# A streaming Conformer layer on one core: VectorE's work is counted with other durations, and block 0's stores are fewer and later

## The chip, the cores and the metric

The kernel runs on one core of a Trainium2 chip. The core has TensorE (PE, matrix products; PEld is its loading of weights), VectorE (DVE), ScalarE (ACT), GpSimd (POOL) and SyncE (SP, which here only issues DMAs); each works through its own list of instructions in order and waits for the others by semaphores. The metric is the device time of one execution in microseconds (us); lower is better.

## The reference, cut to what matters

One layer over a prompt of 2048 tokens and a sample of 32 tokens, all in float32. One projection of the modulated RMSNorm of x feeds two branches, which are gated, added, projected and normed again.

```python
h = rms_norm(x, g_pre) * (1 + scale) + shift            # shift, scale, gate = split(c @ w_mod + b_mod)
a, b, z_conv, q, k, v, z_attn, g_conv, g_attn = split(h @ w_in)
u = a * sigmoid(b)
y = depthwise_conv(u, dw_w, width 31) + dw_b            # per channel, causal; 512 channels
y_conv = (silu(layer_norm(y, ln_g, ln_b)) * silu(z_conv)) @ w_conv_out
o = band_attention(q, k, v, rel_bias)                   # 8 heads of 64, chunks of 64, 8 past chunks
y_attn = (o * silu(z_attn)) @ w_attn_out
merged = sigmoid(g_conv) * y_conv + sigmoid(g_attn) * y_attn
out = x + gate * rms_norm(merged @ w_o, g_post)
```

## The kernel before, in words

Float32 products are made of three products of halves (`mm3`): each operand is split into a rounded part (`wh`, by ACT) and the rest (`wl`, a subtraction on DVE or POOL). The 2048 tokens are taken in four blocks of 512; block 0 also carries the 32 sample tokens, so its matmuls have 272 columns twice where the others have 512. Channels lie on partitions.

A block goes through these stages. **v**: the value projection (`vS`, `vT`). **Attention**: scores (`sps`, `sa`), softmax (`sp`, `mn`, `ll`), transposes (`pt`, `pth`, `ptl`), products (`pv`); between them `fill` places the other projections (`pj`), in the order that `FILL(b)` lists: q and k of the heads, a and b of the convolution in block 0, z, and in block 0 also eight pieces m0 to m7 of the gate row (`mod_part`, `gate_row`). **Gate stage**: sixteen gate projections (`pj`, columns C_GC and C_GA) and four times two products with w_attn_out (`py<-ah`). **Merge stage**: eight products with w_conv_out (`py<-cohi,w`), each behind four transposes of the next block's x (`pxt`). Then w_o in two halves, with the next block's a and b between them.

The convolution's 31 taps for four channel groups are 124 DVE instructions a block (`y<-u,dww,y`, generator `conv`). After the last tap comes a chain: `norm_conv` adds the four groups on POOL (`u<-y`), halves the sum (`lnhi` on ACT, `lnlo` on DVE), takes the mean on PE (`pmean`), subtracts it (`y<-y,pmean`), squares and adds (ACT, POOL), halves again, takes the second `pmean`, forms the reciprocal root on DVE (`rsqrt`, the `u<-u` rows) and multiplies on POOL (`y<-y,u`); then `co` makes tanh and affine on ACT (`th`, `xn`), two products on DVE, and the halves `cohi` (ACT) and `colo` (DVE), which the merge stage reads.

The program writes out each engine's list itself. Two counters decide where a tap stands: `pace.pe` sums an estimate of each matmul as it is written, `pace.dve` (class `Vec`) one of each DVE instruction, and `tick` places taps as long as `pace.dve <= pace.pe + pace.lead`. The norm chain's steps start at times of `pace.pe` too (`YL`). After the gate stage the program writes out what is left of the taps, the chain and `co`, and only then the merge stage. SP's list is not written out by hand; the scheduler orders its DMAs.

Weights come in tiles (`plan`). `weights(i)` splits tile i+2 (`w_parts`, L226 and L228), loads tile i+4 (`w_load`, L216, buffers `raw`) and stores the halves of tile i+1 to DRAM (`w_keep`, L236, 1 MB, on ACT's queue) if it is used again; later blocks load those (`w<-kept`). Which use stores it is `keep_at`. `spill_v` (L603) stores v for the next block.

Of the kernel before, what the change touches and what calls it, by code (L numbers as in the profile page):

```python
# [8 lines left out]
F32 = mybir.dt.float32  # L9
F32R = mybir.dt.float32r  # L10
# [6 lines left out]
P = 128  # L17
D = 1024
# [3 lines left out]
TB = 512  # L22
# [10 lines left out]
C_A, C_B, C_ZC, C_Q, C_K, C_V, C_ZA, C_GC, C_GA = (  # L33
    0, 512, 1024, 1536, 2048, 2560, 3072, 3584, 4608)
# [10 lines left out]
DV = -0.5  # L45
# [8 lines left out]
def FILL(b):  # L54

    part = dict(q=C_Q, k=C_K, a=C_A, b=C_B, z=C_ZA, c=C_ZC, m=C_MOD)
    order = "b0 a0 q1 m0 k1 m1 b1 m2 a1 m3 b2 q2 m4 k2 m5 a2 m6 z0 m7 b3 a3 z1 q3 k3 z2 z3 c0 c1 c2 c3" if b == 0 else \
        "q1 k1 z0 q2 k2 z1 q3 k3 z2 z3 c0 c1 c2 c3"
    return [(int(x[1]), part[x[0]]) for x in order.split()]


def dram(ap, off, dims):
    return bass.AP(tensor=ap.tensor, offset=ap.offset + off, ap=[list(d) for d in dims])
# [54 lines left out]
class Vec:  # L118
# [5 lines left out]
    def __getattr__(self, name):  # L124
        fn = getattr(self.nc.vector, name)

        def call(out, *a, **k):
            n = 1
            for d in out.shape[1:]:
                n *= d  # L130
            ns = 60 + n * (0.6 if name in ("tensor_scalar", "tensor_copy", "memset") else 1.05)
            if name == "scalar_tensor_tensor":
                ns += 70
            ns = max(ns, 200)
            self.pace.dve = max(self.pace.dve, self.pace.pe) + ns / 1e3
            return fn(out, *a, **k)  # L136
        return call
# [3 lines left out]
def mixer_kernel(ctx, tc, x_prompt, x_sample, c_prompt, c_sample, cache_conv, cache_k, cache_v,  # L141
# [4 lines left out]
    G = nc.gpsimd  # L146
    pace = Pace()
    V = Vec(nc, pace)

    def mm(out, lhsT, rhs, start, stop):  # L150
        n = 1
        for d in rhs.shape[1:]:
            n *= d
        pace.pe += (6 + n * 0.4063) / 1e3
        nc.tensor.matmul(out, lhsT=lhsT, rhs=rhs, start=start, stop=stop)  # L155
# [6 lines left out]
    wp = ctx.enter_context(tc.tile_pool(name="wp", bufs=2))  # L162
# [6 lines left out]
    def pp_tile(name):  # L169
        return pp.tile([P, 512], F32, tag="pp", name=name)  # L170
# [18 lines left out]
    for b in range(NB):  # L189
        plan += [w_wide("v", w_in, k, C_V) for k in range(0, KT, 2)]  # L190
        plan += [w_fill(n, c) for n, c in [(0, C_Q), (0, C_K)] + FILL(b)]
        for m in range(0, KT, 2):
            for i in range(2):
                plan += [w_cols(c + (m + i) * P) for c in (C_GC, C_GA)]
            plan.append(w_half("ao", w_attn_out, m))
        plan += [w_half("co", w_conv_out, m) for m in range(0, KT, 2)]
        plan += [w_wide("o", w_o, k, 0) for k in range(0, KT, 2)]
        if b < NB - 1:
            plan += [w_cols(c + ct * P) for ct in range(NCT) for c in (C_B, C_A)]
        plan += [w_wide("o", w_o, k, 512) for k in range(0, KT, 2)]  # L200

    uses = {}
    for i, entry in enumerate(plan):
        uses.setdefault(entry[0], []).append(i)
    keep_at = {key: at[1 if key[0] == "v" else 0] for key, at in uses.items()}
    again = {key for key, at in uses.items() if len(at) > 1}
    raws, halves, kept, used = {}, {}, {}, [0]

# [7 lines left out]
    def w_parts(i):  # L218

        if i < len(plan):  # L220
            key = plan[i][0]
            w = wp.tile([P, 2, 1024], F32R, tag="w", name="w", bufs=3)
            wh, wl = w[:, 0], w[:, 1]
            if i <= keep_at[key]:
                raw = raws.pop(i)
                act(wh, raw, AF.Copy)  # L226
                on_v = pace.dense or pace.idle is None and pace.dve <= pace.pe + DV
                (V if on_v else G).tensor_tensor(wl, raw, wh.bitcast(F32), op=OP.subtract)  # L228
            else:
                nc.sync.dma_start(w.bitcast(F32), kept[key])  # L230
            halves[i] = w
# [6 lines left out]
    def weights(key):  # L238
        i = used[0]
        assert plan[i][0] == key, (i, plan[i][0], key)  # L240
        used[0] += 1
        w_parts(i + 2)
        w_load(i + 4)
        w_keep(i + 1)
        w = halves.pop(i).rearrange("p h (k c) -> p h k c", c=plan[i][1])
        return w[:, 0], w[:, 1]
# [240 lines left out]
    def shape(b):  # L487
        yw = TB + (HIST + TS if b == 0 else 0)
        return TB + (TS if b == 0 else 0), yw, [(0, TB, 0)] + ([(USEP0, USEP0 + TS, TB)] if b == 0 else [])
# [74 lines left out]
    def mod_part(i):  # L564


        n, kp = i // 4, i % 4
        m4, bm, gr = aof[0:4, 3, 0:512], aof[0:2, 2, 0:512], aof[0:2, 1, 0:512]
        if kp == 0:
            nc.sync.dma_start(bm, dram(b_mod, 2 * D + n * 512, [[0, 2], [1, 512]]))  # L570
            nc.sync.dma_start(gr, dram(g_post, n * 512, [[0, 2], [1, 512]]))
        wh, wl = weights(("mod", 2 * kp, (4 + n) * 512))
        pm = pp_tile("pm")
        for kk in range(2):
            mm(pm[0:4], c4[:, 2 * kp + kk, :], wh[:, kk, :], kk == 0, False)
            mm(pm[0:4], c4[:, 2 * kp + kk, :], wl[:, kk, :], False, kk == 1)
            yield
        if kp == 0:
            act(m4, pm[0:4], AF.Copy)
        else:  # L580
            V.tensor_tensor(m4, pm[0:4], m4, op=OP.add)
        if kp == 3:
            pace.start(gate_row(n, m4, bm, gr), 1.5)

    def gate_row(n, m4, bm, gr):
        pg = pp_tile("pg")
        nc.tensor.matmul(pg[0:2], lhsT=sel, rhs=m4, start=True, stop=True)
        yield 1.5
        V.tensor_tensor(bm, pg[0:2], bm, op=OP.add)
        V.tensor_tensor(bm, bm, gr, op=OP.mult)  # L590
        nc.sync.dma_start(gp_d[:, n * 512:(n + 1) * 512], bm)
        gate_done.add(n)
        yield 0.0
# [7 lines left out]
    def spill_v(b, vcur):  # L601
        for t in range(4):
            nc.sync.dma_start(vs_d[b][:, t], vcur[:, t].bitcast(F32))  # L603
            yield 6.0
# [20 lines left out]
    with tc.tile_pool(name="init", bufs=1) as ini:  # L625
        mraw, mparts, m4 = {}, {}, {}
# [63 lines left out]
        with tc.tile_pool(name="x0", bufs=5) as x0:  # L690
# [31 lines left out]
            c2 = vecs[:, 0:16].rearrange("p (a k) -> p k a", a=2)  # L722
# [79 lines left out]
    qls = []  # L802
    for b in range(NB):
        NT, YW, ypieces = shape(b)
# [4 lines left out]
        with tc.tile_pool(name="at", bufs=1) as at:  # L809
# [3 lines left out]
            vcur = at.tile([P, 4, H, P], F32R, name="vcur")  # L813
# [22 lines left out]
                    o = (nvs[0, 0, 512 - TS:512] if t == 4 else nvp[0, 0, t * P:(t + 1) * P])  # L836
                    nc.sync.dma_start(o.rearrange("t h d -> t (h d)"), vo[0:m, 0:512])
            if b < NB - 1:
                pace.start(spill_v(b, vcur), 30.0)

            if b < 2:

                qls.clear()
                for _ in range(2):
                    qls.append(wp.tile([P, 2, TB], F32R, tag="raw", name="ql0") if b else
                               at.tile([P, 2, NT], F32R, tag="ql", name="ql", bufs=2))
                    G.memset(qls[-1][64:128, 0].bitcast(F32), 0.0)
                    G.memset(qls[-1][0:64, 1].bitcast(F32), 0.0)


            att, cvs, ready = {}, {}, set()
# [595 lines left out]
```

## Time and profile before

| | |
|---|---|
| median of three runs | 1754.84 us (1751.86 to 1756.65) |
| the profiled execution | 1752.31 us, of which its span (first to last instruction) 1750.5 us |
| PE busy | 1676.9 us, 96% of the span |
| PE's weight loads | 1428.5 us, 82% |
| DVE, ACT, POOL busy | 1122.5, 633.5, 234.6 us |
| mean granted clock | 0.988 of full speed |

PE is busy nearly all the time, so the profile is read for the stretches in which it is not, and for what ends each of them. The stages can be told by what PE runs: block 0's attention lies at 75 to 330 us of the span, its gate stage at 330 to 458; block 1's gate stage at 761 to 873, block 2's at 1161 to 1272.

### The profile page before, as it was taken

The numbers are of one execution on the slowest core, as the hardware profiler recorded it, in microseconds if no ns is written. First come the engines' busy times: TensorE is split into PE (matmuls) and PEld (weight loads), VectorE is DVE, ScalarE is ACT, GpSimd is POOL, SyncE is SP. The second block draws the span as 40 slices with busy tenths as digits, with TensorE's granted clock in tenths as the row PEclk, the third lists the DMA queues.
The fourth block names the chain that finished last, engine by engine and source line by source line (L and its number), as shares of the span: only waits on it lengthen the run. The fifth ranks groups of instructions, "written<-read, shape, count | busy, mean of one in ns | idle before, by whom it ended". The sixth has DMA issues, their size and how long they took to land.

```text
span 1750.5 us, 23607 instructions
## 1 busy us (share of the span) xinstructions
PE 1676.9 (96%) x9221; PEld 1428.5 (82%) x9221; DVE 1122.5 (64%) x2030; ACT 633.5 (36%) x1218; POOL 234.6 (13%) x174
## 2 busy tenths in 40 slices
PE   6978889999999999999999999999999999999997
PEld 4767779999878788888788888888888888888886
DVE  6457878796737867674544967774543967665423
ACT  6544534424721255522331045531330045531211
POOL 5423332101310000001120000001120000001120
PEclk9998999999999999999999999999999999999999
DMA  8786455776675774465455674465555674455553
GB/s 271 238 286 227 164 200 207 263 277 224 235 261 207 269 276 167 148 226 190 172 217 182 236 272 179 153 221 190 181 216 188 220 262 150 148 181 195 189 192 144
DMA packets 132326, 368.61 MB, mean 211 GB/s; under 512 B 9326, under 2 KB 75050, under 8 KB 101975
## 3 DMA queue, kind: packets, MB, share of 16 engines
q1 hardware_dynamic: 123575, 304.19, 50.4%
q10 hardware_dynamic: 8640, 62.92, 8.8%
q8 instruction: 73, 1.20, 0.3%
q14 instruction: 38, 0.31, 0.1%
HBM read 280.41 MB, written 91.77 MB: 213 GB/s over the span
## 4 chain that ended last, share of the span: by engine, by line
PE 73%; DVE 4%; ACT 2%; DMA 1%; issue 1%; POOL 0%; POOLq 0%; ACTq 0%; DVEq 0%
PE pj L155 41%; PE py L155 9%; PE pv L155 4%; PE op L155 3%; PE sps L155 3%; PE pt L159 3%; PE oT L155 3%; PE oS L155 3%; PE vS L155 2%; PE vT L155 2%; PE oP L155 1%; DMA raw<-in_w_in_dram 1%; DVE pre L136 1%; DMA raw<-in_w_attn_out_dram 1%; PE pxt L159 0%
## 5 line engine op out<-in xcount | busy, mean ns | idle before, releaser
L155 PE MATMUL pj<-hh,w 128*128 128x512 f32 (+1 forms) x4800 | 975.9, 357 | 12.7 <-DVE kk L136 5.4
L155 PEld LDWEIGHTS pj<-hh,w 128*128 128x128 f32 x4800 | 782.6, 190 | 134.7 <-ACT kk L863 4.9
L136 DVE SCALAR_TENSOR_TENSOR y<-u,dww,y 128x512 f32<-128x512 f32 (+1 forms) x480 | 345.9, 781 | 0.5
L1084 ACT ACTIVATE sp<-sp,mn 128x640 f32<-128x640 f32 (+5 forms) x136 | 103.6, 762 | 133.9 <-DVE mn L136 133.9
L1119 ACT ACTIVATE pth<-pt 128x256 fp32r<-128x256 f32 (+4 forms) x184 | 91.8, 500 | 135.1 <-PE pt L159 123.7
L136 DVE TENSOR_TENSOR ptl<-pt,pth 128x256 fp32r<-128x256 f32 (+4 forms) x184 | 104.0, 565 | 28.1 <-ACT pth L1119 26.7
L228 POOL TENSOR_TENSOR w<-raw,w 128x1024 fp32r<-128x1024 f32 x37 | 92.2, 2497 | 177.3 <-ACT w L226 147.7
L136 DVE CUSTOM_DVE_ANT_0 sp<-sps,bias 128x640 f32<-128x640 f32 (+4 forms) x128 | 94.1, 735 | 26.5 <-PE sps L155 25.5
L155 PE MATMUL py<-ah,w 128*128 128x512 f32 (+1 forms) x480 | 96.0, 356 | 6.9 <-DVE t L136 4.8
L226 ACT ACTIVATE w<-raw 128x1024 fp32r<-128x1024 f32 x72 | 75.7, 1052 | 70.5 <-PE py L155 17.0
L155 PEld LDWEIGHTS py<-ah,w 128*128 128x128 f32 x480 | 79.8, 192 | 20.5 <-DVE t L136 5.2
L159 PE MATMUL pt<-ident,sp 128*128 128x128 f32 (+1 forms) x600 | 95.2, 274 | 0.0
L155 PE MATMUL py<-cohi,w 128*128 128x512 f32 (+1 forms) x320 | 90.1, 357 | 1.6 <-DVE mg L136 1.6
L532 POOL TENSOR_TENSOR u<-y 128x512 f32<-128x512 f32 (+1 forms) x4 | 5.3, 1324 | 641.5 <-DVE y L136 591.0
L136 DVE TENSOR_SCALAR sp<-sp,ll 128x640 f32<-128x640 f32 (+5 forms) x136 | 84.5, 621 | 4.8
L155 PE MATMUL sps<-kk,qh 128*128 128x320 f32 (+1 forms) x224 | 70.3, 321 | 9.1 <-DVE mn L136 8.3
L159 PEld LDWEIGHTS pt<-ident,sp 128*128 128x128 f32 (+1 forms) x600 | 69.6, 141 | 3.6 <-issue 1.3
L1347 POOL TENSOR_TENSOR mg<-mg,t 128x512 f32<-128x512 f32 (+1 forms) x32 | 46.4, 1451 | 172.2 <-issue 118.8
L155 PE MATMUL sps<-kk,ql 128*128 128x320 f32 (+1 forms) x224 | 68.5, 313 | 0.0
L1311 ACT ACTIVATE t<-pj 128x512 f32<-128x512 f32 (+1 forms) x40 | 20.7, 517 | 127.6 <-PE pj L155 127.4
L136 DVE SCALAR_TENSOR_TENSOR t<-t,py 128x512 f32<-128x512 f32 (+1 forms) x40 | 23.2, 584 | 67.1 <-PE py L155 67.0
L155 PEld LDWEIGHTS py<-cohi,w 128*128 128x128 f32 x320 | 56.7, 188 | 9.8 <-DVE mg L136 2.3
(255 smaller groups left out, 2250.4 us busy)
## 6 DMA issues: line engine op xcount, KB each, us to landing
w<-kept SPq DMA_DIRECT2D x176, 1024.0 KB, 4.8
kept<-w ACTq DMA_DIRECT2D x60, 1024.0 KB, 4.7
raw<-in_w_in_dram SPq DMA_DIRECT2D x48, 512.0 KB, 4.9
bias<-bias_d SPq DMA_DIRECT2D x32, 320.0 KB, 5.5
xt<-in_x_prompt_dram SPq DMA_DIRECT2D x16, 512.0 KB
wm<-in_w_mod_dram SPq DMA_DIRECT2D x16, 512.0 KB, 7.4
xr<-in_x_prompt_dram SPq DMA_DIRECT2D x16, 512.0 KB, 4.6
vs_d<-vcur SPq DMA_DIRECT2D x12, 512.0 KB
```

The costliest lines, as they stand in the source:

```text
L136: return fn(out, *a, **k)
L155: nc.tensor.matmul(out, lhsT=lhsT, rhs=rhs, start=start, stop=stop)
L159: nc.tensor.transpose(out, in_, idn)
L226: act(wh, raw, AF.Copy)
L228: (V if on_v else G).tensor_tensor(wl, raw, wh.bitcast(F32), op=OP.subtract)
L532: G.tensor_tensor(s2[:, 0:YW], Y[2][:, 0:YW], Y[3][:, 0:YW], op=OP.add)
L1084: self.ex[i] = lambda: act(sp[0:m, 0:nk], sp[0:m, 0:nk], AF.Exp, bias=mn[0:m], scale=-1.0, accum_out=ll[0:m])
L1119: act(self.ph[0:r, f0:f1], pt[0:r, o:o + f1 - f0], AF.Copy)
L1311: pace.run(proj(C_GC + m * P, b, lambda o, c0, c1: act(t1[:, c0:c1], o, AF.Tanh, scale=0.5)))
L1347: G.tensor_tensor(mg, mg, t2, op=OP.add)
```

## The change

It has five parts. (1) `FILL(0)`: m0 to m7 stand later among block 0's projections, and a gate row starts 4.0 instead of 1.5 after its last piece. (2) The count of a DVE instruction in `Vec`: a base of 150 ns for 60 or 70 and no least value, 10% more on long three-operand instructions; and a weight split that goes to POOL now adds 1.0 us to DVE's count. (3) Fourteen tiles (q and k of head pair 0, and twelve of the sixteen gate tiles) are stored at their second use, in block 1, where they are therefore loaded raw and split once more (the gate tiles on DVE); blocks 2 and 3 load the stored halves as before. (4) `spill_v` of block 0 starts 100 instead of 30 after the v stage. (5) Because the `raw` buffers are used again in block 1, blocks 2 and 3 clear their two `ql` tiles anew, on POOL.

```diff
@@ FILL
-    order = "b0 a0 q1 m0 k1 m1 b1 m2 a1 m3 b2 q2 m4 k2 m5 a2 m6 z0 m7 b3 a3 z1 q3 k3 z2 z3 c0 c1 c2 c3" if b == 0 else \
+    order = "b0 a0 q1 k1 b1 m0 a1 m1 b2 m2 q2 m3 k2 m4 a2 m5 z0 m6 b3 m7 a3 z1 q3 k3 z2 z3 c0 c1 c2 c3" if b == 0 else \
@@ Vec
-            ns = 60 + n * (0.6 if name in ("tensor_scalar", "tensor_copy", "memset") else 1.05)
-            if name == "scalar_tensor_tensor":
-                ns += 70
-            ns = max(ns, 200)
+            ns = 150 + n * (0.59 if name in ("tensor_scalar", "tensor_copy", "memset") else 1.05)
+            if name == "scalar_tensor_tensor" and n >= 512:
+                ns += 0.1 * n
@@ mixer_kernel
+    def gate(key):
+        return key[0] == "in" and key[1] >= C_GC
+
+    def twice(key):
+        if gate(key):
+            return (key[1] - C_GC) % D >= 2 * P
+        return key[0] == "v" or key in (("in", C_Q), ("in", C_K))
...
-    keep_at = {key: at[1 if key[0] == "v" else 0] for key, at in uses.items()}
+    keep_at = {key: at[1 if twice(key) else 0] for key, at in uses.items()}
@@ w_parts
-                on_v = pace.dense or pace.idle is None and pace.dve <= pace.pe + DV
+                on_v = pace.dense or gate(key) and i > uses[key][0] or pace.idle is None and pace.dve <= pace.pe + DV
                 (V if on_v else G).tensor_tensor(wl, raw, wh.bitcast(F32), op=OP.subtract)
+                if not on_v:
+
+                    pace.dve = max(pace.dve, pace.pe) + 1.0
@@ mod_part
-            pace.start(gate_row(n, m4, bm, gr), 1.5)
+            pace.start(gate_row(n, m4, bm, gr), 4.0)
@@ block
-                pace.start(spill_v(b, vcur), 30.0)
-
-            if b < 2:
-
-                qls.clear()
-                for _ in range(2):
...
+                pace.start(spill_v(b, vcur), 100.0 if b == 0 else 30.0)
+
+
+            qls.clear()
+            for _ in range(2):
...
```

The table of counts and the delays move instructions, and three places show how. The first is PE's list at the end of block 0's gate stage. Before, the rows are these (`py<-ah` is the product with w_attn_out, `pmean` the mean of the norm chain, `pxt` the first instruction of the merge stage):

```order
L155 MATMUL pj<-hh,w 128x272 x15
L155 MATMUL py<-ah,w 128x272 x48
L155 MATMUL pj<-hh,w 128x272 x45
L155 MATMUL pmean<-lnhi,onesr 128x512
L155 MATMUL pmean<-lnlo,onesr 128x512
L155 MATMUL pmean<-lnhi,onesr 128x32
L155 MATMUL pmean<-lnlo,onesr 128x32
L155 MATMUL pj<-hh,w 128x272 x147
L155 MATMUL py<-ah,w 128x272 x48
L159 MATMUL pxt<-ident,xt 128x128 x4
```

Of the change the same place reads so (its line numbers are lower by one here):

```order
L154 MATMUL pj<-hh,w 128x272 x192
L154 MATMUL py<-ah,w 128x272 x48
L154 MATMUL pmean<-lnhi,onesr 128x512
L154 MATMUL pmean<-lnlo,onesr 128x512
L154 MATMUL pmean<-lnhi,onesr 128x32
L154 MATMUL pmean<-lnlo,onesr 128x32
L154 MATMUL pmean<-lnhi,onesr 128x512
L154 MATMUL pmean<-lnlo,onesr 128x512
L154 MATMUL pmean<-lnhi,onesr 128x32
L154 MATMUL pmean<-lnlo,onesr 128x32
L158 MATMUL pxt<-ident,xt 128x128 x4
```

The second mean stood 195 matmuls ahead of the merge stage and the first still further; now both stand behind the last `py<-ah`, with nothing between them and the merge stage. On DVE's list of the change the same stretch reads as follows (the last taps `y<-u,dww,y`, weight splits `w<-raw`, the four gate products `t<-t,py`, then the chain):

```order
L135 SCALAR_TENSOR_TENSOR y<-u,dww,y 128x574 x6
L135 TENSOR_TENSOR w<-raw,w 128x1024
L135 SCALAR_TENSOR_TENSOR y<-u,dww,y 128x574 x4
L135 TENSOR_TENSOR w<-raw,w 128x1024
L135 SCALAR_TENSOR_TENSOR t_4539<-t_4539,py 128x272 x2
L135 SCALAR_TENSOR_TENSOR t_4665<-t_4665,py 128x272 x2
L135 TENSOR_TENSOR lnlo<-u,lnhi 128x574
L135 TENSOR_TENSOR y<-y,pmean 128x512
```

The chain's first DVE step (`lnlo`) stands behind the last four gate products, which read the last `py`; before, the last taps stood in the third of the four groups of the gate stage. Block 0's attention holds 58 taps instead of 63, its gate stage 66 instead of 61.

The second place is PE's list over the last groups of block 1's gate stage, before:

```order
L155 MATMUL pj<-hh,w 128x512 x69
L155 MATMUL pmean<-lnhi,onesr 128x512
L155 MATMUL pmean<-lnlo,onesr 128x512
L155 MATMUL pj<-hh,w 128x512 x12
L155 MATMUL py<-ah,w 128x512 x24
L155 MATMUL pj<-hh,w 128x512 x96
L155 MATMUL py<-ah,w 128x512 x24
L159 MATMUL pxt<-ident,xt 128x128 x4
```

and of the change:

```order
L154 MATMUL pj<-hh,w 128x512 x78
L154 MATMUL pmean<-lnhi,onesr 128x512
L154 MATMUL pmean<-lnlo,onesr 128x512
L154 MATMUL pj<-hh,w 128x512 x18
L154 MATMUL py<-ah,w 128x512 x24
L154 MATMUL pmean<-lnhi,onesr 128x512
L154 MATMUL pmean<-lnlo,onesr 128x512
L158 MATMUL pxt<-ident,xt 128x128 x4
```

Here the second mean moves from 156 matmuls ahead of the merge stage to right in front of it, the first to 42 ahead. In blocks 2 and 3 the second mean stands 114 matmuls ahead (it was 189), the first 183 (it was 258).

The third place is SP's list early in block 0's attention (`bias_d` are the eight heads' bias tables in DRAM, written from `lrow` and then patched from `msk`; `vs_d` is v's store). Before:

```order
L880 DMA zcb<-in_cache_k_dram 128x4x128
L570 DMA aof<-in_b_mod_dram 2x512
L571 DMA aof<-in_g_post_dram 2x512
L603 DMA vs_d_121<-vcur 128x1024 x3
L837 DMA out_dram<-vo 32x512
L617 DMA bias_d_106<-lrow_d 128x768
L216 DMA raw<-in_w_in_dram 128x8x128
L603 DMA vs_d_121<-vcur 128x1024
```

and of the change:

```order
L889 DMA zcb<-in_cache_k_dram 128x4x128
L627 DMA bias_d_106<-lrow_d 128x768
L580 DMA aof<-in_b_mod_dram 2x512
L581 DMA aof<-in_g_post_dram 2x512
L627 DMA bias_d_107<-lrow_d 128x768
L629 DMA bias_d_106<-msk 64x64
L630 DMA bias_d_106<-msk 64x64
L627 DMA bias_d_108<-lrow_d 128x768
L847 DMA out_dram<-vo 32x512
L629 DMA bias_d_107<-msk 64x64
L630 DMA bias_d_107<-msk 64x64
L223 DMA raw<-in_w_in_dram 128x8x128
```

The stores of v no longer stand ahead of this weight load; two more table writes do, and the patches, each of which waits for its table.

## Rows read from the trace of the kernel before

**Rows 1.** Busy time by stage: length, engines, granted clock, DMA share.

```profile
75.00:330.00 255.00, 223.03 (x1640) 202.97 (x1639) 186.61 (x391) 121.21 (x280) 83.17 (x40) 0.95 0.64 217
330.00:458.00 128.00, 120.89 (x946) 119.66 (x944) 102.06 (x147) 50.29 (x88) 19.43 (x14) 0.99 0.75 270
...
761.00:873.00 112.00, 109.63 (x473) 88.50 (x473) 70.29 (x109) 27.41 (x46) 11.54 (x9) 1.00 0.57 207
873.00:1161.00 288.00, 287.45 (x1479) 242.33 (x1478) 186.20 (x348) 102.01 (x200) 14.60 (x17) 1.00 0.55 199
```

**Rows 2.** PE's waits in block 0's attention, 75 to 330 us: total, times, longest.

```profile
PE sps L155 <- DVE mn L136: 7.4, 3, 6.7
PE pj L155 <- DVE kk L136: 5.4, 2, 4.4
```

**Rows 3.** Timelines at 85 to 102 us: SP, ACT, and PE after its wait.

```profile
70.52 1.31 SPq L617 DMA_DIRECT2D bias_d<-lrow_d  x1
...
78.50 0.45 SPq L619 DMA_DIRECT2D bias_d<-msk  x1
...
85.14 1.31 SPq L216 DMA_DIRECT2D raw<-in_w_in_dram  x1
...
97.32 1.06 ACT L226 ACTIVATE w<-raw 128x1024 fp32r<-128x1024 f32 x1 [6.86 <-DMA raw<-in_w_in_dram]
...
101.27 0.69 PE L155 MATMUL sps<-kk,qh 128*128 128x384 f32 x1 [6.74 <-DVE mn L136]
...
102.08 2.92 PE L155 MATMUL pj<-hh,w 128*128 128x272 f32 x12
```

**Rows 4.** Taps on DVE in block 0's attention, 75 to 330 us: busy, mean ns.

```profile
L136 DVE SCALAR_TENSOR_TENSOR y<-u,dww,y 128x574 f32<-128x574 f32 x60 | 59.0, 984 | 0.2
```

**Rows 5.** DVE's timeline over block 0's gate stage, the chain's steps.

```profile
412.58 0.75 DVE L136 TENSOR_TENSOR lnlo<-u,lnhi 128x574 fp32r<-128x574 f32 x1
...
414.57 2.86 DVE L136 TENSOR_TENSOR y<-y,pmean 128x512 f32<-128x512 f32 x8
...
427.40 0.76 DVE L136 TENSOR_TENSOR lnlo<-u,lnhi 128x574 fp32r<-128x574 f32 x1 [1.68 <-ACT lnhi L515]
429.48 0.79 DVE L136 TENSOR_SCALAR u<-pmean 128x512 f32<-128x512 f32 x2 [1.32 <-PE pmean L155]
...
435.81 0.72 DVE L136 SCALAR_TENSOR_TENSOR u<-u 128x544 f32<-128x544 f32 x1
...
442.00 1.28 DVE L136 SCALAR_TENSOR_TENSOR xn<-th,xn 128x544 f32<-128x544 f32 x1 [2.10 <-ACT xn L1261]
...
446.49 0.72 DVE L136 SCALAR_TENSOR_TENSOR colo<-xn,cohi 128x544 fp32r<-128x544 f32 x1
...
455.89 0.72 DVE L136 SCALAR_TENSOR_TENSOR colo<-xn,cohi 128x544 fp32r<-128x544 f32 x1
...
457.82 0.44 DVE L136 SCALAR_TENSOR_TENSOR t<-t,py 128x272 f32<-128x272 f32 x1 [0.53 <-PE py L155]
```

**Rows 6.** POOL's adds and multiplications of the same chain.

```profile
418.71 3.43 POOL L547 TENSOR_TENSOR u<-u 128x574 f32<-128x574 f32 x2 [0.44 <-ACT u L546]
436.68 8.73 POOL L560 TENSOR_TENSOR y<-y,u 128x512 f32<-128x512 f32 x8 [14.54 <-DVE u L136]
```

**Rows 7.** Block 1's chain after its second mean: DVE, POOL, PE.

```profile
834.56 0.69 DVE L136 TENSOR_SCALAR u<-pmean 128x512 f32<-128x512 f32 x1 [4.71 <-PE pmean L155]
...
840.57 0.69 DVE L136 SCALAR_TENSOR_TENSOR u<-u 128x512 f32<-128x512 f32 x1
...
853.48 0.69 DVE L136 SCALAR_TENSOR_TENSOR colo<-xn,cohi 128x512 fp32r<-128x512 f32 x1 [0.76 <-ACT cohi L1271]
...
861.63 0.69 DVE L136 SCALAR_TENSOR_TENSOR colo<-xn,cohi 128x512 fp32r<-128x512 f32 x1 [0.70 <-ACT cohi L1271]
...
841.34 5.06 POOL L560 TENSOR_TENSOR y<-y,u 128x512 f32<-128x512 f32 x4 [17.10 <-DVE ss L136]
...
850.85 16.91 PE L155 MATMUL pj<-hh,w 128*128 128x512 f32 x72 [2.37 <-DVE t L136]
```

More of the change, by code (lines that the diff above doesn't have):

```diff
@@ L838, in mixer_kernel @@
             if b < NB - 1:
-                pace.start(spill_v(b, vcur), 30.0)
-            if b < 2:
-                qls.clear()
-                for _ in range(2):
[L845 to L848, printed above, removed]
+                pace.start(spill_v(b, vcur), 100.0 if b == 0 else 30.0)
+            qls.clear()
+            for _ in range(2):
+                qls.append(wp.tile([P, 2, TB], F32R, tag="raw", name="ql0") if b else
+                           at.tile([P, 2, NT], F32R, tag="ql", name="ql", bufs=2))
+                G.memset(qls[-1][64:128, 0].bitcast(F32), 0.0)
+                G.memset(qls[-1][0:64, 1].bitcast(F32), 0.0)
             att, cvs, ready = {}, {}, set()
```

## The prediction, made before the changed kernel ran

> **What bounds the kernel now.** I read the page first: PE is busy 96% of the span, so only what stops PE or slows its clock is worth anything, and nearly every stop lies in the first 500 us. The table by stage [rows 1] says where: in block 0's attention PE is idle for 255.0 - 223.0 = 32.0 us, and its granted clock is 0.95, a loss of about 0.05 x 255 = 12.8 us more. In block 0's gate stage it is idle for 7.1 us, in block 1's for 2.4 us. Later gate stages are full.
>
> Next the waits of the attention stage [rows 2]: PE waits for DVE almost always, and the longest wait, 6.7 us, is for `mn`, the row minimum of the first scores. The timelines show what is behind it [rows 3]. A weight load issued at 85.14 us reaches ACT's split only at 97.32, after 6.86 us in which ACT could do nothing else; the first exponential stands behind that split on ACT's list, DVE's next step behind the exponential, and PE starts again at 101.27. Its clock then has dropped to the lower of its two levels: twelve matmuls of 272 columns take 2.92 us, where at the full clock they take half of that. I charge 2 us for each restart after a long stop.
>
> Last the chain of block 0's gate stage [rows 5, 6]. Its last half (`colo`) ends at 455.89 + 0.72 = 456.6 us, and the last gate product of the branch runs on DVE at 457.82: the chain is ready some 1.4 us before PE needs it. So before, the norm chain costs PE nothing, but it has no room in block 0. In block 1 the last `colo` ends at 862.3 [rows 7], ten us before the stage ends at 873.
>
> **The change, part by part.** *The count of taps* is what decides. A tap of 574 columns is counted as 60 + 574 x 1.05 + 70 = 733 ns before, and 150 + 603 + 57 = 810 now. In the attention stage taps last 984 ns on average [rows 4], so there the new count is nearer; but each is charged relative to PE's count, and in the gate stage a tap of the trace lasts 0.73 us (the chain's instructions of the same size take 0.72 to 0.75 [rows 5]), so there the old count was right and the new one spreads the taps out. The order shows the result: block 0's chain now stands behind the last product of the gate stage, on PE and on DVE, and the merge stage right behind it. PE's list is in order, so nothing can fill the gap. What it costs is the chain's own length from the end of the last gate product, summed from the rows of before:
>
> the last gate product and `lnlo` on DVE, 0.44 + 0.75 = 1.2; the mean, 429.48 - (427.40 + 0.76) = 1.3; from the first subtraction at 414.57 to the end of POOL's adds at 418.71 + 3.43 = 422.14, 7.6 [rows 5, 6]; the second halving, two steps of 0.76, 1.5; the second mean, 1.3; the reciprocal root, 429.48 to 435.81 + 0.72 = 436.5, 7.0; from there to the first `colo` at 446.49, 10.0 as placed, of which I take off 1.7 for a weight split and a gate step that lay in between, 8.3; to the last `colo` at 455.89, 9.4, less 0.6 for the same reason, 8.8; and that one's 0.7. Sum 37.7 us. While the last groups are made PE can already do the four transposes and nine of each twelve products of the first merge step, about 1.7 us. The stall is 36 us. Its bounds: 33 if the steps close up better than that, 44 if they lie as they lie now (412.58 to 456.6).
>
> Block 1: the second mean now stands behind the last gate product too. DVE's last product and `lnlo`, 2 x 0.69 = 1.4; the mean, 1.3; the root, 834.56 to 840.57 + 0.69 = 841.3, 6.7; one multiplication on POOL (5.06 / 4 = 1.3), two steps on ACT, two on DVE and a half on ACT, about 5.2; three more groups at the pace of the last ones, (861.63 - 853.48) / 3 = 2.72, 8.2; the last 0.7 [rows 7]. Sum 23.5, less 2.5 us of PE work that goes ahead: 21 us, between 18 and, as placed now from 834.56 to 862.3, 28. Blocks 2 and 3: there 114 matmuls of 0.233 us (16.91 us for 72, [rows 7]), 26.6 us, stay between the second mean and the merge stage; the same chain without its first step needs 6.7 + 5.2 + 8.2 + 0.7 = 20.8. It fits with 6 us to spare and costs nothing; if that cover went it would be some us in each. Two long stalls also mean two restarts at the lower clock, 2 x 2 = 4 us. Together the change loses 36 + 21 + 4 = 61 us.
>
> *Stores, their order, and m0 to m7* can give back at most what PE loses now: 32.0 + 12.8 in the attention stage, 7.1 and about 1.3 of clock in block 0's gate stage, 2.4 in block 1's: 55.6 us. How much of it? The 6.7 us wait hangs on the load issued at 85.14. Without v's stores and two tile stores the transfer is quicker, but the load now stands behind two more table writes and their patches, and a patch waits for its table: a write issued at 70.52 had its patch at 78.50, 8 us later [rows 3]. The write that stood at about 80 thus puts the load's issue at about 90 instead of 85; if it then lands in half the 12 us it took, it comes 1 to 2 us sooner. I take 2 us here, 2 for the next loads, 7 for waits on DVE and clock (five taps of 0.98 fewer, and the gate row's sums out of the way of the early scores), 3 of the gate stage's 7.1 (twelve stores of 1 MB leave it) and the 2.4 of block 1, which was a gate product behind the next block's statistics: 16 us. A loss here is possible too: DVE does the same work in this stage, and the load may come later; 10 us at worst, the size of the first two waits together.
>
> The Trainium skill ("DMA: Bandwidth & Descriptors", section "Issuing engines are not separate DMA queues") says that DMAs of all issuing engines run on the same 16 DMA engines and interleave, so that another engine's queue saves only issue time. By that, stores on ACT's queue hold up loads on SP's, and taking them out would end the whole 6.7 us wait with its restart, 9 us in place of my 2: the sum would be 7 us less. The row of 85.14 agrees that loads are slow in that stretch; whose bytes did it, no row says.
>
> *The rest is hidden.* Fourteen more splits in block 1 are 14 steps on ACT of 1.06 us [rows 3] and about as much on DVE, in a stage where ACT is busy for 27 of 112 us and DVE for 70 [rows 1]; without that cover they would cost 14 us. Twelve stores of 1 MB move into that stage, whose DMA share is 0.57; if loads were held up there, the price is one such late load, some 7 us. The clearing of `ql` in blocks 2 and 3 lies on POOL, which from block 1's merge stage to the end of block 2's attention is busy for 14.6 of 288 us [rows 1].
>
> **Sum.** 1752.3 (the profiled execution, 1750.5 of it span) + 61 - 16 = 1797. The median of the runs shown is 2.5 us above that execution, so I say 1798.
>
> **The rivals.** *B, the stores caused the attention's waits.* The pile-up on DVE after 101 us would start with the late load, and without it most of the 55.6 us goes, say 45: 1752 + 61 - 45 = 1768. For it: the waits begin with a load that took 12 us. Against: the load's new place on SP, and that DVE is busy for 187 of 255 us in this stage with the same work. The rule of the Trainium skill above (same page) points this way too. *C, the load comes later still* and PE waits longer in the attention stage, by 10 us, with the rest gained: 1752 + 61 - 5 + 10 = 1818. *D, not slower:* DVE, which has only 102 of 128 us of work in block 0's gate stage [rows 1], runs ahead of the program's count, so that the chain is done before PE arrives. Then nothing is lost, 16 is gained: 1737. Against it stands one row of the order: `lnlo` follows the four gate products, which need PE's last results. It decides if `lnlo` could start before them; by the lists it can't. *E, gain and loss cancel:* all 55.6 us come back against 61 or less: 1757.
>
> **How the numbers follow.** The forecast (its own range 1783 to 1812) has 0.73, B 0.11, C 0.08, D 0.03, E 0.05. The range from 1772 to 1816 takes in the stalls' bounds (-6, +15) and the gain's (0 to 30); it leaves out D, E, half of B and half of C. A difference under 0.3%, 5.3 us, can't be told from none here. Faster is D: 0.03. Same is E and the lower end of B: 0.05. Slower: 0.92.
>
> **What would show it.** In the new profile PE should have one idle stretch of 33 to 44 us between block 0's last `py<-ah` and the first `py<-cohi`, broken only by the two means, with `colo` as its last releaser, and one of 18 to 28 us at the same place of block 1; none in blocks 2 and 3. In block 0's attention PE's idle time should be 20 to 32 us, and a wait for `mn` of several us should be left near 100 us. The prediction is wrong if the chain's steps start before the last gate product ends, or if the attention stage gives back more than 30 us; the first would show as short waits at `pmean`, the second as a granted clock near 1.00 there.

## The result and the profile after

The changed kernel takes 1796.6 us (median of four runs, 1791.25 to 1798.44) beside 1755.42 us of the kernel before (1751.86 to 1756.65): a ratio of 1.0232, 95% interval 1.0208 to 1.0256. It is slower, near the 1798 us that the prediction gave. The profiled execution took 1794.92 us.

The page's head:

```profile
span 1793.1 us, 23661 instructions
PE 1683.4 (94%) x9221; PEld 1429.6 (80%) x9221; DVE 1125.6 (63%) x2044; ACT 646.9 (36%) x1232; POOL 238.0 (13%) x182
```

PE's longest waits over the whole span (total, times, longest):

```profile
PE py L154 <- ACT cohi L1280: 31.6, 8, 13.1
...
PE pj L154 <- DVE kk L135: 7.5, 1, 7.5
PE pmean L154 <- ACT lnhi L525: 7.3, 1, 7.3
```

Against the kernel before PE is busy for 6.5 us more and idle for 36 us longer, and the wait that leads the list did not exist: `cohi`, the merge stage's operand, eight times, which is four times each in blocks 0 and 1.

Where the time went is read best by marks on PE's list, since both kernels run the same matmuls. The table takes the start of the first matmul of a kind (or the end of the last `py<-ah`) from PE's timeline in each kernel and shows the stretches between them, in us.

| stretch | before | after | difference |
|---|---|---|---|
| start to block 0's first `py<-ah` | 350.40 | 344.53 | -5.87 |
| to the end of block 0's last `py<-ah` | 107.38 | 99.81 | -7.57 |
| to the first `py<-cohi` | 0.20 | 24.21 | +24.01 |
| to block 1's first `vS` | 126.11 | 135.65 | +9.54 |
| to block 1's first `py<-ah` | 196.38 | 198.68 | +2.30 |
| to the end of its last `py<-ah` | 92.86 | 90.04 | -2.82 |
| to its first `py<-cohi` | 0.18 | 15.47 | +15.29 |
| to block 2's first `vS` | 114.88 | 123.25 | +8.37 |
| to the end of the last matmul | 752.23 | 751.91 | -0.32 |
| sum | 1740.62 | 1783.55 | +42.93 |

Nearly all of the loss, 57.2 of 59.5 us, stands at the two places that the prediction named: around block 0's and block 1's first `py<-cohi`, ahead of it and in the merge stage behind it. PE's timeline after block 0's gate stage (start, duration, instruction; in brackets the idle time ahead and its releaser):

```profile
438.18 6.16 PE L154 MATMUL py<-ah,w 128*128 128x272 f32 x48
444.18 0.39 PE L154 MATMUL pmean<-lnhi,onesr 128*128 128x512 f32 x1
445.54 0.50 PE L154 MATMUL pmean<-lnlo,onesr 128*128 128x512 f32 x1 [0.97 <-DVE lnlo L135]
...
453.46 0.80 PE L154 MATMUL pmean<-lnhi,onesr 128*128 128x512 f32 x1 [7.29 <-ACT lnhi L525]
...
455.12 1.11 PE L158 MATMUL pxt<-ident,xt 128*128 128x128 f32 x4
468.55 0.59 PE L154 MATMUL py<-cohi,w 128*128 128x272 f32 x1 [12.31 <-ACT cohi L1280]
...
477.36 0.60 PE L154 MATMUL py<-cohi,w 128*128 128x272 f32 x1 [1.32 <-ACT cohi L1280]
...
480.56 0.52 PE L154 MATMUL py<-cohi,w 128*128 128x272 f32 x2
480.92 0.29 PE L154 MATMUL py<-colo,w 128*128 128x272 f32 x1
```

Both means wait, then the first product of the merge stage, then the first of each further channel group. DVE's timeline has the chain itself:

```profile
444.38 0.44 DVE L135 SCALAR_TENSOR_TENSOR t<-t,py 128x272 f32<-128x272 f32 x1 [1.05 <-PE py L154]
444.74 0.75 DVE L135 TENSOR_TENSOR lnlo<-u,lnhi 128x574 fp32r<-128x574 f32 x1
...
446.07 2.87 DVE L135 TENSOR_TENSOR y<-y,pmean 128x512 f32<-128x512 f32 x8 [0.59 <-PE pmean L154]
453.44 0.76 DVE L135 TENSOR_TENSOR lnlo<-u,lnhi 128x574 fp32r<-128x574 f32 x1 [4.50 <-ACT lnhi L525]
455.08 0.79 DVE L135 TENSOR_SCALAR u<-pmean 128x512 f32<-128x512 f32 x2 [0.89 <-PE pmean L154]
...
461.41 0.72 DVE L135 SCALAR_TENSOR_TENSOR u<-u 128x544 f32<-128x544 f32 x1
...
468.53 0.91 DVE L135 SCALAR_TENSOR_TENSOR colo<-xn,cohi 128x544 fp32r<-128x544 f32 x1 [0.80 <-ACT cohi L1280]
...
477.34 0.73 DVE L135 SCALAR_TENSOR_TENSOR colo<-xn,cohi 128x544 fp32r<-128x544 f32 x1 [0.78 <-ACT cohi L1280]
```

From 444.38 to 477.34 + 0.73 = 478.07 it is 33.7 us; before, the same steps were spread from 412.58 to 456.6 [rows 5], with PE at work beside them. In block 1 the second mean and all that follows it are late (PE, then DVE's last gate product and last `colo`):

```profile
892.77 0.40 PE L154 MATMUL pmean<-lnhi,onesr 128*128 128x512 f32 x1
894.39 0.50 PE L154 MATMUL pmean<-lnlo,onesr 128*128 128x512 f32 x1 [1.22 <-DVE lnlo L135]
894.73 0.60 PE L158 MATMUL pxt<-ident,xt 128*128 128x128 f32 x4
908.39 0.80 PE L154 MATMUL py<-cohi,w 128*128 128x512 f32 x1 [13.07 <-ACT cohi L1280]
...
916.54 0.79 PE L154 MATMUL py<-cohi,w 128*128 128x512 f32 x1 [0.77 <-ACT cohi L1280]
...
921.67 0.39 PE L154 MATMUL py<-colo,w 128*128 128x512 f32 x1
...
893.04 0.69 DVE L135 SCALAR_TENSOR_TENSOR t<-t,py 128x512 f32<-128x512 f32 x1 [2.18 <-PE py L154]
...
916.52 0.69 DVE L135 SCALAR_TENSOR_TENSOR colo<-xn,cohi 128x512 fp32r<-128x512 f32 x1 [0.70 <-ACT cohi L1280]
```

The stages, answering to [rows 1] (length, engines, granted clock, DMA share); the last two are the chains of block 0 and block 1:

```profile
75.00:330.00 255.00, 223.64 (x1671) 205.08 (x1670) 178.68 (x388) 122.71 (x282) 83.83 (x37) 0.95 0.63 218
330.00:444.40 114.40, 111.11 (x887) 110.74 (x885) 81.41 (x115) 33.90 (x57) 5.15 (x3) 1.00 0.51 173
444.40:478.10 33.70, 8.42 (x22) 4.92 (x21) 20.62 (x34) 15.20 (x26) 11.44 (x11) 0.58 0.02 8
...
892.90:917.20 24.30, 7.71 (x17) 3.28 (x15) 17.35 (x24) 9.20 (x14) 5.37 (x4) 0.59 0.12 43
```

In block 0's attention PE is idle for 31.4 us, before 32.0, at the same clock. A wait of some 7 us is there as well, a little earlier and with another cause. ACT's timeline:

```profile
83.54 1.04 ACT L233 ACTIVATE w<-raw 128x1024 fp32r<-128x1024 f32 x1
91.22 0.35 ACTq L246 DMA_DIRECT2D kept<-w  x1
91.62 0.39 ACT L871 ACTIVATE kk<-pj 64x272 fp32r<-64x272 f32 x1 [7.04 <-DMA bias_d<-lrow_d]
```

Before, ACT waited for a late raw load [rows 3]. Now it stands in front of the issue of a store. The store reads the two halves that ACT and POOL made; in the program it also waits for a DMA semaphore that it shares with a bias-table write:

```
L246 DMA kept_863<-w 128x2048 [waits DMAHW3_49,Pool_49]
```

In the trace the table write issued at 85.38 us and this store report their landing on the same semaphore. So ACT, and with it the head's `kk`, waits 7.04 us for a transfer that neither needs, and PE waits for `kk` for 7.5 us.

### The profile page after: what moved, and what is told of

It is laid out like the page before. It is cut to its first block, busy times and chain, and to the rows that moved or that the text cites. A ratio compares the mean times of both kernels' runs of the same rounds, so it can differ in the third digit from the quotient of the medians.

```text
span 1793.1 us, 23661 instructions
## 1 busy us (share of the span) xinstructions
PE 1683.4 (94%) x9221; PEld 1429.6 (80%) x9221; DVE 1125.6 (63%) x2044; ACT 646.9 (36%) x1232; POOL 238.0 (13%) x182
## 4 chain that ended last, share of the span: by engine, by line
PE 61%; DVE 2%; DMA 1%; issue 1%; ACT 1%; POOL 0%; POOLq 0%; DVEq 0%; ACTq 0%; SPq 0%
PE pj L154 34%; PE py L154 7%; PE pv L154 4%; PE sps L154 3%; PE pt L158 3%; PE op L154 2%; PE oT L154 2%; PE oS L154 2%; PE vS L154 1%; PE vT L154 1%; PE oP L154 1%; DMA w<-kept 1%; DMA kept<-w 0%; DVE xn L135 0%; PE pxt L158 0%
## 5 line engine op out<-in xcount | busy, mean ns | idle before, releaser
L154 PE MATMUL py<-cohi,w 128*128 128x512 f32 (+1 forms) x320 | 96.9, 375 | 33.1 <-ACT cohi L1280 31.6
L233 ACT ACTIVATE w<-raw 128x1024 fp32r<-128x1024 f32 x86 | 90.2, 1052 | 88.7 <-PE py L154 25.6
L135 DVE TENSOR_TENSOR w<-raw,w 128x1024 fp32r<-128x1024 f32 x49 | 61.7, 1260 | 68.2 <-ACT w L233 68.2
L135 DVE TENSOR_SCALAR sp<-sp,ll 128x640 f32<-128x640 f32 (+5 forms) x136 | 76.1, 560 | 4.8
L1320 ACT ACTIVATE t<-pj 128x512 f32<-128x512 f32 (+1 forms) x40 | 20.7, 518 | 147.5 <-PE pj L154 147.5
L1321 ACT ACTIVATE t<-pj 128x512 f32<-128x512 f32 (+1 forms) x40 | 20.7, 517 | 118.9 <-PE pj L154 118.9
```

The costliest lines, as they stand in the source:

```text
L1320: pace.run(proj(C_GC + m * P, b, lambda o, c0, c1: act(t1[:, c0:c1], o, AF.Tanh, scale=0.5)))
L1321: pace.run(proj(C_GA + m * P, b, lambda o, c0, c1: act(t2[:, c0:c1], o, AF.Tanh, scale=0.5)))
```

## The experiments

The theory: the loss is where the last taps and the norm chain stand, and no part of it is the stores or the new splits as such. The rivals: the stores and splits cost it; or the taps' new count costs DVE something wherever they stand. A measure of the place is how many steps down PE's list the first `py<-cohi` stands from the last `pmean<-lnhi`: before 201 in block 0 and 162 in block 1, after 6 and 6 (the rest of the mean, the four `pxt` and the product itself). The expectations call this the matmuls behind the mean.

**e1, the new count alone**, on the kernel before (201 becomes 6 in block 0, 162 becomes 75 in block 1):

```diff
-            ns = 60 + n * (0.6 if name in ("tensor_scalar", "tensor_copy", "memset") else 1.05)
...
+            ns = 150 + n * (0.59 if name in ("tensor_scalar", "tensor_copy", "memset") else 1.05)
...
+                if not on_v:
+                    pace.dve = max(pace.dve, pace.pe) + 1.0
```

> The kernel before with only the new count (durations and the 1.0 us for a split on GpSimd). In its order block 0's two means stand behind the last gate product, as in the changed kernel, but in block 1 75 matmuls still stand between the second mean and the merge stage, 75 x 0.235 = 17.6 us, more than the 14.0 us that lay between that mean and the first cohi in the changed kernel's trace. Theory (the exposed chain is the loss): block 0 loses 32 us as measured, block 1 nothing: 1755 + 32 = 1787 us, or 1776 if the 11 us that the stages ahead of the chain gained come from the count as well. Rival (the stores and the new splits are the loss): 1755 us.

Measured: 1780.75 us, ratio 1.0152 (1.0135 to 1.0169), between the two figures of the theory. The stretch from the last `py<-ah` to block 0's first `py<-cohi` is 24.21 us, as in the changed kernel, and the gate stage ahead of it is 6.75 us shorter. Block 1 was expected to lose nothing. Its merge stage loses 5.9 us and its gate stage gains 2.4: two of the later channel groups still make PE wait, 3.0 us with their `colo`, and PE's granted clock then falls to half for 3.4 us:

```profile
896.55 0.48 PE L154 MATMUL py<-cohi,w 128*128 128x512 f32 x1
...
899.73 0.50 PE L154 MATMUL py<-cohi,w 128*128 128x512 f32 x1 [1.26 <-ACT cohi L1273]
...
902.45 0.49 PE L154 MATMUL py<-cohi,w 128*128 128x512 f32 x1 [1.27 <-ACT cohi L1273]
```

Hence most of block 1's loss needs the count and the new splits together; with both, the mean stands another 69 matmuls later. By the program it is the splits' own entries in DVE's count of block 1's gate stage that push the taps on.

**e2, all parts but the count:**

> The changed kernel with the old count and without the 1.0 us; order of the pieces, stores, spill and the clearing stay. Block 0's second mean again has 201 matmuls behind it, block 1's 108. Theory: no chain is exposed, so what is left is the gain of the other parts, 0 to 12 us: 1743 to 1755 us, middle 1748. Rival (stores and splits are the loss): near 1790 us.

Measured: 1744.71 us, ratio 0.9948 (0.9933 to 0.9963). The rest of the change is a gain of some 9 us, almost all ahead of block 0's first `py<-ah` (341.12 us, before 350.40); block 1's start gives 4.9 us back, its gate stage gains 2.5. The gate stage of block 0 gains 1.25 us only.

**e3, the new durations without the 1.0 us for a split on POOL:**

> The changed kernel without the 1.0 us that a split on GpSimd adds; the new durations stay. Block 0's second mean has 54 matmuls behind it, 54 x 0.116 = 6.2 us, block 1's order is that of the changed kernel. Theory: block 0's stall shrinks from 32 by 6.2 us and by the first half of the chain, some 9 us, to about 15 us, block 1 keeps its 21: 1797 - 17 = 1780 us. Rival (the durations do it all): 1797 us.

Measured: 1783.56 us, ratio 1.0171 (1.0156 to 1.0186). Block 0 loses 5.2 us from its first `py<-ah` to the first `py<-cohi` and 9.95 behind it, the 15 us expected; the stretch ahead of block 1's merge stage is that of the changed kernel, 15.48 us. So the charge for POOL's splits sets only how far block 0's chain falls behind.

**e4, e7 and e10, the whole change with the taps allowed to run ahead.** First 26 us from the end of the attention stage on in blocks 0 and 1, then only until the merge stage, then 12 us in place of 26 in block 1:

```diff
-            pace.lead = LEAD
+            pace.lead = LEAD + (26.0 if b < 2 else 0.0)                        # e4, e7
+            pace.lead = LEAD + (26.0 if b == 0 else 12.0 if b == 1 else 0.0)   # e10
...
             while "co" not in ready:
                 pace.pe += 0.5
                 pace.tick()
+            pace.lead = LEAD                                                   # e7, e10
```

> The changed kernel, whole, but from the end of the attention stage on taps may run 26 us further ahead of PE's count in blocks 0 and 1 (one number). Block 0's second mean then has 201 matmuls behind it, block 1's 354. Theory: the stall is a matter of where the last taps stand, and the whole loss goes with it: 1743 to 1755 us, middle 1748; below the kernel before if what the attention stage gained stays. Rival (DVE has not the time for the taps so early, so PE waits for its gate products instead): above 1765 us.

Measured: 1806.08 us, ratio 1.0298 (1.0282 to 1.0313). The expectation failed. Both stalls ahead of the merge stages are gone (0.19 us in each block), but three other stretches lose some 20 us each: both merge stages and block 1's v and attention stages. The next run tests whether the next block's taps, which now stand earlier, are the reason. PE's waits of this run:

```profile
PE op L154 <- DVE u L135: 20.4, 3, 10.4
PE pmean L154 <- ACT lnhi L525: 14.7, 1, 14.7
PE oT L154 <- DVE w L135: 12.9, 1, 12.9
```

> The changed kernel with the same 26 us of lead, now only from the end of the attention stage to the start of the merge stage; from there on the lead is the old one, so that the next block's taps stand where the changed kernel has them. 201 and 192 matmuls stand behind the second means of blocks 0 and 1. Theory (the run with the lead kept on lost its 61 us behind the merge stage, to the next block's taps, and nothing in the gate stages): no stall in either block, and the time falls to that of the old count, 1742 to 1750 us, middle 1745. Rival (the taps' lead itself costs as much as the chain): 1780 us or more.

Measured: 1762.32 us, ratio 1.0053 (1.0034 to 1.0072), 44 us less than e4, and 17 above what was expected. The three stretches of e4 are back within 3 us of the kernel before, and no chain is exposed, but at the start of block 1's gate stage 42 taps stand in one run ahead of a weight split, and PE waits for that (DVE from 775.8 us on, with the last 31 of them, then PE):

```profile
775.79 20.62 DVE L135 SCALAR_TENSOR_TENSOR y<-u,dww,y 128x512 f32<-128x512 f32 x31
796.33 1.21 DVE L135 TENSOR_TENSOR w<-raw,w 128x1024 fp32r<-128x1024 f32 x1
...
797.60 2.93 PE L154 MATMUL pj<-hh,w 128*128 128x512 f32 x6 [13.27 <-DVE w L135]
```

> The changed kernel, whole, with a lead of 26 us in block 0's gate stage and 12 us in block 1's, the old lead elsewhere. 201 and 105 matmuls stand behind the second means, and in block 1 the burst of taps that held up a weight split by 13.3 us with a lead of 26 us is 14 us shorter. Theory (the place of the last taps is the whole loss): no stall of either kind, 13.7 us less than with 26 us in both: 1748 us, 1745 to 1752. Rival (taps counted in the new way cost DVE something in any place): above 1756 us.

Measured: 1750.16 us, ratio 0.9982 (0.9971 to 0.9993). With 105 matmuls behind block 1's second mean neither stall is left, and the time is 46 us below that of the changed kernel, of which only the leads differ. The place of the taps is the loss, but for the 5 us above e2 that remain: 3.7 in block 0's gate stage, where PE's longest wait for `t` is 5.3 us in place of 3.0, 2.4 in block 1's, and smaller differences of both signs elsewhere.

**e5, e6 and e8, where the other parts' 9 us come from.** e5 is the kernel before with the new order of pieces; e6 with the stores, the spill and the clearing; e8 is e2 with q and k of head pair 0 stored at the first use:

```diff
-        return key[0] == "v" or key in (("in", C_Q), ("in", C_K))
+        return key[0] == "v"
```

> The kernel before with only the new order of the pieces (m0 to m7 later, gate row 4.0 after its last piece). The old count with all the other parts gave 8.8 us, nearly all of it before the first product with w_attn_out (341.1 us in place of 350.4). Theory (the early m pieces and their gate rows crowd DVE and delay the first scores): most of it, 5 to 9 us, comes from the order: 1746 us. Rival (the stores out of the stage free the loads): nothing from the order, 1753 us.

> The kernel before with the fewer and later stores, the later spill and the clearing, but the old count and the old order of the pieces. Theory (the order gives the gain): the attention stage gains 0 to 4 us, block 1 loses about 2 us as with all parts: 1753 us. Rival (the stores give it): 1745 us.

> All parts but the count, and q and k of head pair 0 again stored at their first use; the twelve gate tiles stay at the second. With all parts but the count block 1's start lost 4.9 us against the kernel before, of which 3.1 us one wait for a kept weight. Theory (two more raw loads at block 1's start shift SP's list, so that the loads of kk and vh run ahead of it): the wait goes, 1741 us. Rival (the wait comes from other transfers): 1745 us, or above if the two stores of 1 MB more in block 0 cost something.

Measured: e5 1752.38 us, ratio 0.9994 (0.9984 to 1.0003), no difference that can be told; e6 1748.24, 0.9967 (0.9954 to 0.9979); e8 1751.12, 0.9988 (0.9976 to 0.9999). The theory that the order gives the gain is wrong. The stores alone give 5 us, less than the rival said; with the order on top it is 8.8, and two of the 60 stores moved back into block 0 (e8) take 6 us of that away. In e8 the 3.1 us wait of block 1 is gone, as expected, but the time is 10 us above the 1741 expected. What is common to these runs is a hold-up of ACT at the issue of an early store, at other places and for other lengths: 4.95 us in e2, 5.3 in e5, 2.7 in e6, 3.5 in e8, 7.04 in the changed kernel. In the kernel before no store holds ACT for more than some 1.0 us in this stage.

**e9, e11 and e12, the stores issued by SP**, on e2, on the kernel before and on the whole change:

```diff
-            nc.scalar.dma_start(kept[plan[i][0]], halves[i].bitcast(F32))
+            nc.sync.dma_start(kept[plan[i][0]], halves[i].bitcast(F32))
```

> All parts but the count, with the kept stores issued by SyncE instead of ScalarE. In the trace with all parts but the count ScalarE stands 4.95 us at 84 to 89 us in front of the issue of a kept store, which waits for the bias-table write to land, and PE's wait of 5.44 us at 90.9 us follows from it. Theory (ScalarE is held up by the issue, not by the transfer): that wait falls under 2 us and the time by 2 to 5 us, 1741 us. Rival (the data come late whoever issues, or SyncE's loads now stand behind the stores): 1745 us or more.

Measured: 1734.4 us, ratio 0.9897 (0.9874 to 0.9919), the fastest version of the study, more than the theory gave. ACT now goes straight from the split to `kk`:

```profile
87.07 1.05 ACT L234 ACTIVATE w<-raw 128x1024 fp32r<-128x1024 f32 x1
88.14 0.39 ACT L869 ACTIVATE kk<-pj 64x272 fp32r<-64x272 f32 x1
```

and PE's wait there falls from 5.44 to 0.51 us. The wait for a kept weight in block 1 is gone too.

> The kernel before with nothing changed but the engine that issues the kept stores, SyncE in place of ScalarE. Theory (ScalarE's hold-ups at the issue are what the gain of 10 us from this edit came from, whatever the number of stores): 1753 - 10 = 1743 us, with PE's idle time in block 0's attention below 27 us. Rival (with all the stores in block 0, SyncE's loads stand behind them): 1753 us or more.

Measured: 1739.0 us, ratio 0.992 (0.9905 to 0.9935), with all stores still in block 0. PE is idle for 23.4 of the 255 us of block 0's attention, before 32.0:

```profile
75.00:330.00 255.00, 231.56 (x1724) 212.44 (x1723) 194.96 (x409) 126.11 (x286) 84.33 (x40) 0.96 0.69 235
```

The time is the expected one, the reason is not. In the kernel before, ACT's long waits for a DMA in this stage are for two late raw loads, and not for the issue of a store (total, times, longest):

```profile
ACT w L226 <- DMA raw<-in_w_in_dram: 6.9, 1, 6.9
ACT w L226 <- DMA raw<-in_w_mod_dram: 4.7, 1, 4.7
```

With the stores on SP's list both waits are gone.

> The changed kernel, whole, with the kept stores issued by SyncE. Its order on PE and VectorE is that of the changed kernel, so both chains stay exposed. Theory (the stores' issue and the exposed chains have nothing to do with each other): the stalls stay at 24 and 15 us ahead of the merge stages, and the time is 1797 - 10 = 1787 us. Rival (a late ScalarE lengthens the chain): stalls shorter by several us and below 1775 us.

Measured: 1784.34 us, ratio 1.0176 (1.0159 to 1.0193). The stretches ahead of the merge stages are 24.22 and 15.47 us, unchanged to 0.01 us; the gain lies ahead of block 0's chain and, with 3.0 us, at block 1's start, where the wait for a kept weight is gone. The exposed chains do not depend on who issues the stores.

## Why the prediction was right, point by point

*The chains, 37.7 and 23.5 us by the sums.* Measured 33.7 us in block 0, by the steps that were named and in their order, and 24.2 in block 1 (893.04 to 916.52 + 0.69 = 917.21). In block 0 half of the terms hold within 0.2 us: product and `lnlo` 1.1 (1.2), the root from 455.08 to 462.1 7.0 (7.0), the last three groups 8.8 (8.8), the last `colo`. The others were too long: the two means 0.6 and 0.9 in place of 1.3 each, from the first subtraction to the end of the second halving 8.1 in place of 9.1, root to first `colo` 6.4 in place of 8.3. The steps lie closer here, where the other work of PE and DVE no longer stands between them.

*The stalls of 36 and 21 us and the restarts of 2 us each.* By the stage rows PE is idle for 33.70 - 8.42 = 25.3 us in block 0's chain and for 24.30 - 7.71 = 16.6 in block 1's. Besides block 0's shorter chain, the term that was mis-sized is PE's own work inside the chain, put at 1.7 and 2.5 us: it is 8.4 and 7.7, made of the means, the transposes and the products of each channel group, which PE starts as soon as that group is ready, most of it at half the clock. So the sign that was named did not come as stated: from the last `py<-ah` to the first `py<-cohi` it is 24.21 and 15.47 us, not 33 to 44 and 18 to 28, and the last releaser is `cohi`, not `colo`.

The restarts were mis-sized the other way. After PE has stood nearly idle, its granted clock falls to the lower of its two levels, half of the full clock, in the trace from 450.1 to 480.8 us and from 897.2 to 921.1; matmuls of 512 columns take 0.79 us at 916.54 and 0.39 at 921.67. In block 1's merge stage 8.37 - 2.31 = 6.1 us are left that no wait explains, in block 0's 9.54 - 4.7 = 4.8. Half of the work that PE does there at the lower level, 5.2 and 3.7 us, is the clock's; about 1 us in each stays unexplained. All four stretches together cost 57.2 us, less some 1.2 for the two means that used to stand in block 0's gate stage: 56 us, forecast 61. That it comes so near is in part luck: too much idle time and too little for the clock.

*The gain of 16 us.* Measured: 5.9 ahead of the first `py<-ah` (forecast 2 + 2 + 7 = 11), 7.6 - 1.2 = 6.4 in block 0's gate stage (3), 2.8 in block 1's (2.4): 15 us. The total is right, but its reasons are not, which is luck. Ahead of the first `py<-ah` PE's idle time fell by 1.4 us only; the rest is PE's own work, 296.8 us in place of 301.3, at a granted clock of 0.97 in place of 0.96. The gate stage's gain was put down to the stores that leave it; e1, which keeps them all, has it (6.75 us), and e2, which has the fewer stores, has not (1.25). This points to the chain's departure: its steps on DVE and ACT no longer stand among the gate products, so the gain would belong to the loss. It is not the only way to that gain: e9 and e11, with the chain in its old place, shorten this stage by 4.8 us. In the attention stage, the load was expected 1 to 2 us sooner, with a wait for `mn` left near 100 us; the longest wait for `mn` now is 1.3 us, the wait that is left is for `kk`, and its cause, a store's issue, was in no part of the prediction.

*The count of taps.* The prediction read 984 ns [rows 4] as a tap's duration in the attention stage and 0.73 us in the gate stage. In the trace a tap of 574 columns lasts 0.81 us in both: 52 of the 60 in the attention stage take 0.82 us or less, and the mean comes from the other 8, of 1.5 to 2.9 us, each of which runs beside a weight split on POOL. The 0.73 us is what a tap takes in a run of taps, where each starts before the last has ended. That is the figure that a count needs there. The run of 31 taps of 512 columns in e7 agrees: 20.62 / 31 = 0.67 us, for which the old count has 668 ns and the new one 739. So the conclusion, that the old count was right in the gate stage and the new one spreads the taps out, holds.

*Hidden parts.* Blocks 2 and 3 lost nothing (-0.32 us from block 2's `vS` to the end), as said. The 14 splits were called free; as instructions they are (e2 has them, and block 1's gate stage is 2.5 us shorter), but the changed kernel beside e1 shows that together with the new count they put block 1's chain at the end of the stage. The "one late load" allowed for in block 1 came, as a wait for a kept weight, 2.76 us of the table's +2.30. Sum: 56 - 15 + 2.3 - 0.3 = 43, forecast 45.

*The rivals.* D, the chain done early, is refuted by the rows of block 0. C, ten us more of waiting in the attention stage, and E, all 55.6 us gained, did not come either: idle time there is 31.4 us, before 32.0. B, that the stores cause the attention's waits, was given 0.11 and is half right: e11 wins 13 us by the stores' issuer alone, with as many stores as before; but the changed kernel, which kept ACT as issuer, did not collect it. The chance of 0.05 for "same" is E's alone, although the prediction says that it holds the lower end of B too.

The Trainium skill ("DMA: Bandwidth & Descriptors", section "Issuing engines are not separate DMA queues") says that a second issuing engine saves only issue time, usually little beside the transfer. In the runs here the issuer mattered more: the issue itself takes ACT 0.35 us, but in the changed kernel what stood behind it waited 7.04 us, since an issue that waits for a semaphore holds the rest of the engine's list, and with the stores on SP that kernel is some 10 us faster against the kernel before (e12).

What stays open: in e11 the late raw load of the kernel before [rows 3] is gone as well, and no run tells whether the stores' place on SP or a semaphore that they share moved it; so the cause of e11's gain is open beyond those two loads. And why order and stores together give more than the sum of both is not settled beyond ACT's changing hold-ups.

## What to carry to other kernels

A count that places work on one engine in step with another's should be read by what it leaves between the last step of a chain and its first reader: the number of PE's instructions there, times their duration, set beside the chain's own length. The chains' lengths, summed from rows of the kernel before, came out here within 4 us. For the stall, PE's own work inside the chain has to be taken off, at the clock that is granted there. When the durations of a count are changed, the lead that keeps the chain covered changes with them, and has to be set again for each stage: with leads of 26 and 12 us the change takes 1750 us where it took 1797, 5 us above the same change with the old count (e10 and e2). And a DMA issue on an engine with work behind it is a wait like any other: look for idle time that ends in a transfer that the next instruction does not read.

## What the runs showed of the hardware

In both stalls, in which PE had only a few matmuls, the granted clock fell to its lower level (0.58 and 0.59 on the mean of the two chains) and cost 4.8 and 6.1 us more behind the first `py<-cohi`, beyond the waits and with about 1 us in each not explained; the prediction had put it at 2 from the shorter stop near 100 us [rows 3]. A tap on DVE that ran beside a weight split on POOL took up to 2.9 us in place of 0.81 (8 of 60 taps in block 0's attention before). The same 60 stores of 1 MB cost 13 us less when SP issued them, at a higher DMA share in the stage (0.69, before 0.64).
